# Two small buffers of a hybrid block's memory norm, allocated ahead of the normalized input

## The chip, the core and the metric

The kernel runs on one core of one Trainium2 chip. The metric is the time of one execution in device microseconds, as the median of several runs. One more execution was recorded by the hardware profiler; all rows below come from it. PE is TensorE's matmul stream and PEld its weight loads, DVE is VectorE, ACT is ScalarE, POOL is GpSimd, and SP is the engine that issues the loads of the weights.

## What is computed

Two layers act on 512 tokens of width 1024, with 256 memory tokens. Each layer adds three blocks to `x`:

```python
for l in range(DEPTH):                       # DEPTH = 2
    x = x + hybrid_mixer(rms_norm(x, norm_mix_g[l]), ...)
    x = x + memory_cross_attention(rms_norm(x, norm_xattn_g[l]),
                                   rms_norm(mem, norm_mem_g[l]), ...)
    x = x + conv_gated_mlp(rms_norm(x, norm_ffn_g[l]), ...)
return rms_norm(x, final_norm_g)
```

The mixer projects the normalized input to fourteen groups of columns and feeds three branches: chunked retention, a gated delta rule (a triangular solve and a scan over chunks) and dilated window attention. Three gates of width 1024 weigh their outputs, and `w_out` follows. Cross attention has four heads over the memory. The feed-forward block projects up to 2 x 2816, runs a short causal convolution, multiplies silu of one half by the other, and projects down. All is float32.

## The kernel before

**Split matmuls.** Every float32 operand of a projection is held as two parts in the type fp32r: a rounded high part and the low rest. `mm3` (lines 210 to 213) makes a product of three matmuls: high x high, low x high, high x low. For an activation the parts are `xgh` and `xgl` (normalized input), `mh`/`ml` (merged branches), `rh`/`rl`, `gh`/`gl`, `odil` (branch outputs), `ah`/`al` (feed-forward) and `mgh`/`mgl` (memory). For a weight they are `wh`, made by ScalarE in line 200, and `wl`, made by VectorE in line 201, from a slab `w` that SP loads.

**Which operand moves.** `fm_tile` (line 215) has the weight part as the loaded operand (128 x 128) and streams 512 tokens of the activation past it; `fm_one` uses it for one output tile with one slab, which is 8 x 3 = 24 matmuls, and `fm_group` for four output tiles at once. Its outputs have the names `gate`, `ua`, `uu`, `up`, `g`, `dqk`, `rqk` and `xq` where the activation is `xgh`/`xgl`, and `wo`, `dn`, `dl`, `y`, `xo`, `km` where it is another. `tm_group` (line 260) turns this round: a block of 128 tokens of the activation is the loaded operand, and the weight parts stream. Its outputs are `rva`, `rvb`, `rg`, `z`, `dv` (from `xgh`/`xgl`; the 512 columns of `dv` take every fourth token) and `vm` (from `mgh`/`mgl`). In the trace a matmul is written `out<-moving,loaded` with the names in either order.

**Order.** The instructions are put in order by a scheduler when the program is built; the parts that prepare weights are marked to come first, and the evictions of PSUM soon.

**Places in SBUF.** Single tiles lie in the pool `pp` in the order of their allocation: the constants `c`, the parameters `par`, `xgh` and `xgl` (lines 173, 174), and at line 1094 `mrow` and `mrc`. Behind them come the regions (`r0` to `r10`, `q0` to `q2`) that hold `mh`, `rh`, `ah`, `mgh` and the other large tiles in turn, and then the slabs and small tiles. Each start is rounded up to 32 bytes. `mrc` takes the 1 / rms of the memory tokens by partition, and `mrow` the same by column; `memory_norm` fills them once, in layer 0, and `cross` reads them in both layers.

Of the kernel before, what the change touches and what calls it, by code (L numbers as in the profile page):

```python
# [9 lines left out]
F32 = mybir.dt.float32  # L10
# [8 lines left out]
P = 128  # L19
T = 512  # L20
M = 256
# [78 lines left out]
def tile_hybrid(ctx, tc, xT, memT, pos, wts, cst, kst, prm, rows, outT):  # L100
# [4 lines left out]
    pp = ctx.enter_context(tc.tile_pool(name="pp", bufs=1))  # L105
# [57 lines left out]

    c = pp.tile([P, C_N], F32, name="c")
    par = pp.tile([P, P_N], F32, name="par")
    with tc.high_priority(offset=2000000):
        nc.scalar.dma_start(par[:, :P_GC], prm[:, :P_GC])
    ident = c[:, C_ID:C_ID + P]
# [922 lines left out]

        return Two(mh), Two(ml)

    mrow, mrc = pp.tile([P, M], F32, name="mrow"), pp.tile([P, 2], F32, name="mrc")

    def mem_load(kt):
        mraw = tg(f"mem{kt}", (2, M))
        G.dma_start(mraw, memT[:, kt:kt + 2, :])
        return mraw
# [409 lines left out]
```

## Time and profile before

| | us |
|---|---|
| median of 3 runs | 2123.67 |
| lowest and highest run | 2121.73, 2125.4 |
| the profiled execution | 2123.01 |
| its span, first to last instruction | 2121.2 |

Of the span PE is busy for 98%, its weight loads, which overlap with it, for 81%, DVE for 64%, ACT for 43% and POOL for 20%. The program reads 198.55 MB from HBM, nearly all of it weights, at a mean of 97 GB/s. A matmul's duration in the profile runs from its start to a modelled end, and the next one starts before that; so the sum of durations says little, and the distance from one start to the next says what a matmul costs.

### The profile page before, as it was taken

The page shows a single profiled execution, that of the slowest core. Times are in us where ns is not written, and L with a number is a line of the kernel's source. Part 1 is how long each engine was busy: PE and PEld are TensorE (multiplying, and loading weights), DVE is VectorE, ACT ScalarE, POOL GpSimd, SP SyncE. Part 2 cuts the span into 40 slices and gives each one's busy share as a digit, 9 for nine tenths or more (in the row PEclk, how much of TensorE's full clock was granted, in tenths as well). Part 3 has the DMA queues.
Part 4 walks back from the last instruction along what each step waited for, and adds up shares of the span by engine and source line. Part 5 has one row for each costly group of instructions (what it writes and reads, how often), then busy time and mean ns, then how long its engine had stood idle before and what let it go on. Part 6 is the DMA issues. An engine that isn't in the chain of part 4 may idle for free.

```text
span 2121.2 us, 28468 instructions
## 1 busy us (share of the span) xinstructions
PE 2076.4 (98%) x10537; PEld 1710.2 (81%) x10537; DVE 1363.0 (64%) x2478; ACT 918.7 (43%) x1879; POOL 422.4 (20%) x438
## 2 busy tenths in 40 slices
PE   7999999999999999999999999999999999999997
PEld 6787888777787888888887889888788878888886
DVE  6789666444767875476547986834447677645754
ACT  4653424443445543244445533344335454423433
POOL 6842220013010311011115231200211021101112
PEclk9999999999999999999999999999999999999998
DMA  4332222235232323222332231223342322223232
GB/s 154 125 105 81 77 78 81 79 115 149 86 116 78 100 90 96 98 94 94 119 122 85 95 109 52 74 80 110 110 119 90 109 90 90 92 98 99 90 95 84
DMA packets 64874, 207.32 MB, mean 98 GB/s; under 512 B 7896, under 2 KB 15552, under 8 KB 63968
## 3 DMA queue, kind: packets, MB, share of 16 engines
q1 hardware_dynamic: 60240, 191.89, 28.5%
q0 software_dynamic: 4144, 13.54, 2.2%
q8 instruction: 82, 1.34, 0.3%
q14 instruction: 56, 0.46, 0.1%
q10 hardware_dynamic: 352, 0.09, 0.0%
HBM read 198.55 MB, written 6.93 MB: 97 GB/s over the span
## 4 chain that ended last, share of the span: by engine, by line
PE 84%; DVE 8%; DMA 3%; issue 2%; ACT 2%; POOL 1%; SPq 0%; ACTq 0%; DVEq 0%; POOLq 0%
PE gate L212 4%; PE gate L213 4%; PE gate L211 4%; PE uu L213 4%; PE ua L213 4%; PE ua L212 4%; PE uu L212 4%; PE ua L211 4%; PE uu L211 4%; PE dn L211 3%; PE dn L213 3%; PE dn L212 3%; DVE wl L201 2%; PE dqk L213 2%; PE dqk L212 2%; PE dqk L211 2%
## 5 line engine op out<-in xcount | busy, mean ns | idle before, releaser
L200 ACT ACTIVATE wh<-w 128x512 fp32r<-128x512 f32 (+2 forms) x690 | 429.4, 624 | 844.2 <-PE uu L212 123.0
L201 DVE TENSOR_TENSOR wl<-w,wh 128x512 fp32r<-128x512 f32 (+2 forms) x690 | 512.3, 745 | 335.3 <-ACT wh L200 315.1
L213 PE MATMUL gate<-xgh,wl 128*128 128x512 f32 x384 | 153.5, 400 | 1.4 <-DVE wl L201 1.4
L211 PE MATMUL gate<-xgh,wh 128*128 128x512 f32 x384 | 153.0, 399 | 0.6 <-ACT wh L200 0.6
L212 PE MATMUL gate<-xgl,wh 128*128 128x512 f32 x384 | 152.9, 398 | 0.0
L301 POOL TENSOR_TENSOR acc<-acc,sq 128x512 f32<-128x512 f32 (+1 forms) x48 | 66.1, 1377 | 356.6 <-ACT sq L300 297.7
L211 PE MATMUL ua<-xgh,wh 128*128 128x512 f32 x320 | 126.6, 396 | 0.0
L212 PE MATMUL ua<-xgl,wh 128*128 128x512 f32 x320 | 126.6, 396 | 0.0
L213 PE MATMUL ua<-xgh,wl 128*128 128x512 f32 x320 | 126.6, 396 | 0.0
L211 PE MATMUL uu<-xgh,wh 128*128 128x512 f32 x320 | 126.6, 396 | 0.0
L212 PE MATMUL uu<-xgl,wh 128*128 128x512 f32 x320 | 126.6, 396 | 0.0
L213 PE MATMUL uu<-xgh,wl 128*128 128x512 f32 x320 | 126.6, 396 | 0.0
L1243 POOL TENSOR_TENSOR fya<-fya,fyu 128x512 f32<-128x512 f32 x44 | 73.0, 1659 | 230.3 <-DVE fyu L1226 228.5
L211 PE MATMUL dn<-ah,wh 128*128 128x512 f32 x264 | 102.7, 389 | 0.0
L212 PE MATMUL dn<-al,wh 128*128 128x512 f32 x264 | 102.7, 389 | 0.0
L213 PE MATMUL dn<-ah,wl 128*128 128x512 f32 x264 | 99.8, 389 | 0.0
L213 PEld LDWEIGHTS gate<-xgh,wl 128*128 128x128 f32 x384 | 72.2, 188 | 19.1 <-DVE wl L201 1.9
L212 PEld LDWEIGHTS gate<-xgl,wh 128*128 128x128 f32 x384 | 72.2, 188 | 17.7 <-issue 1.2
L211 PEld LDWEIGHTS gate<-xgh,wh 128*128 128x128 f32 x384 | 72.2, 188 | 17.2 <-ACT wh L200 0.9
L401 POOL TENSOR_TENSOR rot<-rot,tab 128x512 f32<-128x512 f32 x32 | 49.0, 1536 | 175.9 <-DVE rot L400 162.4
L213 PE MATMUL g<-xgh,wl 128*128 128x512 f32 x192 | 77.3, 404 | 3.2 <-DVE wl L201 3.0
L211 PE MATMUL g<-xgh,wh 128*128 128x512 f32 x192 | 77.3, 402 | 1.2 <-ACT wh L200 1.2
(513 smaller groups left out, 5145.1 us busy)
## 6 DMA issues: line engine op xcount, KB each, us to landing
w<-in_wts SPq DMA_DIRECT2D x330, 512.0 KB, 3.5
mem<-in_memT POOLq DMA_DIRECT2D x12, 256.0 KB, 3.4
attn<-gd_rd POOLq DMA_DIRECT2D x2, 1024.0 KB, 5.9
tab<-tabs_d POOLq DMA_DIRECT2D x4, 512.0 KB, 4.2
x<-in_xT SPq DMA_DIRECT2D x2, 1024.0 KB, 6.5
dr<-sh_rd SPq DMA_DIRECT2D x16, 128.0 KB, 4.3
x_d<-x SPq DMA_DIRECT2D x8, 256.0 KB, 4.2
x<-x_d SPq DMA_DIRECT2D x2, 1024.0 KB, 6.7
```

The lines of the kernel that those rows point to most:

```text
L200: S.activation(wh[:, :m], w[:, o:o + m], AF.Copy)
L201: V.tensor_tensor(wl[:, :m], w[:, o:o + m], wh[:, :m], ALU.subtract)
L211: PE.matmul(out, lhsT=lh, rhs=rh, start=start, stop=False)
L212: PE.matmul(out, lhsT=lh, rhs=rl, start=False, stop=False)
L213: PE.matmul(out, lhsT=ll, rhs=rh, start=False, stop=stop)
L301: eng.tensor_tensor(acc, acc, sq, ALU.add)
L401: G.tensor_tensor(t, t, tab[:, 1, :], ALU.mult)
L1243: G.tensor_tensor(ya, ya, yu, ALU.mult)
```

## The change

Line 1094 moves up, to stand in front of `xgh` and `xgl`. What is computed, the names and the shapes stay.

```diff
     c = pp.tile([P, C_N], F32, name="c")
     par = pp.tile([P, P_N], F32, name="par")
+    mrow, mrc = pp.tile([P, M], F32, name="mrow"), pp.tile([P, 2], F32, name="mrc")
     with tc.high_priority(offset=2000000):
         nc.scalar.dma_start(par[:, :P_GC], prm[:, :P_GC])
...
-    mrow, mrc = pp.tile([P, M], F32, name="mrow"), pp.tile([P, 2], F32, name="mrc")
-
     def mem_load(kt):
```

The order of the instructions in the built program is the same on all five engines, row by row, and so are the semaphores that they wait for; only numbers in names and line numbers differ. What differs is the place of four tiles in each partition of SBUF, in bytes from its start:

| tile | bytes | start before | start after | start mod 2048, before and after |
|---|---|---|---|---|
| `c` | 1552 | 16512 | 16512 | |
| `par` | 2080 | 18080 | 18080 | |
| `xgh` | 16384 | 20160 | 21216 | 1728, 736 |
| `xgl` | 16384 | 36544 | 37600 | 1728, 736 |
| `mrow` | 1024 | 52928 | 20160 | |
| `mrc` | 8 | 53952 | 21184 | |
| `r7` (`rh` and others), the first region | 8192 | 53984 | 53984 | 736, 736 |
| `r1` and `r10` (`mh`, `ah` and others) | 8192 | 103136, 140000 | the same | 736, 736 |
| `r5` (`mgh` and others) | 8192 | 86752 | 86752 | 736, 736 |
| `wh`, the first of 3 | 2048 | 164576 | 164576 | 736, 736 |
| `wl`, the first of 3 | 2048 | 170720 | 170720 | 736, 736 |

Within `xgh` and `xgl` the eight slices of 512 tokens are 2048 bytes apart, and so are the slices in the regions; the three `wh` are 2048 bytes apart, and the three `wl`; a load of 128 weights starts at a multiple of 512 bytes in its tile.

## Rows read from the trace of the kernel before

**Rows 1.** The page: busy us (share of the span), and PE's granted clock in 40 slices.

```profile
PE 2076.4 (98%) x10537; PEld 1710.2 (81%) x10537; DVE 1363.0 (64%) x2478; ACT 918.7 (43%) x1879; POOL 422.4 (20%) x438
...
PEclk9999999999999999999999999999999999999998
```

**Rows 2.** PE's waits: line, for what: us in total, times, longest us.

```profile
PE rva L211 <- ACT wh L200: 8.5, 3, 7.9
PE nfin_rp L1206 <- DVE rc L287: 5.2, 2, 4.7
PE g L213 <- DVE wl L201: 3.0, 2, 2.3
PE rg L212 <- DVE wl L201: 2.4, 2, 1.4
PE z L212 <- DVE wl L201: 2.2, 2, 1.6
...
PE xo L211 <- DVE pt L1171: 0.3, 2, 0.2
```

**Rows 3.** PE by windows: us, PE busy (x), PEclk, DMA share, GB/s.

```profile
723.06:728.66 5.60, 5.60 (x25) 1.00 0.33 97
...
568.34:573.78 5.44, 5.44 (x25) 1.00 0.32 99
```

**Rows 4.** Four tiles: duration min/median/max in ns, first and last start, forms.

```profile
L212 PE MATMUL ua<-xgl,wh x320: 395/396/397, 723.3 to 2038.4; 128*128 128x512 f32 x160
...
L211 PE MATMUL wo<-mh,wh x128: 389/389/389, 568.3 to 1648.9; 128*128 128x512 f32 x128
...
L211 PE MATMUL dn<-ah,wh x264: 389/389/395, 823.9 to 2073.7; 128*128 128x512 f32 x132
...
L213 PE MATMUL y<-rh,wl x64: 389/389/501, 350.6 to 1472.2; 128*128 128x512 f32 x64
```

**Rows 5.** Groups of matmuls by shape: xcount | busy us, mean ns | idle before.

```profile
L212 PE MATMUL gate<-xgl,wh 128*128 128x512 f32 x384 | 152.9, 398 | 0.0
...
L212 PE MATMUL ua<-xgl,wh 128*128 128x512 f32 x320 | 126.6, 396 | 0.0
...
L212 PE MATMUL g<-xgl,wh 128*128 128x512 f32 x192 | 76.7, 399 | 0.0
...
L212 PE MATMUL xq<-xgl,wh 128*128 128x512 f32 x64 | 25.5, 398 | 0.0
...
L213 PE MATMUL rg<-wh,xgl 128*128 128x512 f32 x64 | 25.2, 394 | 0.0
```

**Rows 6.** PE by windows: `rg`, `vm`, `rvb`, `km`, `dv`, `rva`.

```profile
1079.89:1088.75 8.86, 8.86 (x39) 1.00 0.31 90
1695.90:1699.76 3.86, 3.86 (x18) 1.00 0.34 98
1159.86:1170.82 10.96, 10.96 (x96) 1.00 0.38 98
611.86:617.73 5.87, 5.87 (x50) 1.00 0.34 96
328.54:336.81 8.27, 8.27 (x36) 1.00 0.42 132
1066.94:1072.91 5.97, 5.97 (x50) 1.00 0.28 89
```

**Rows 7.** All engines by windows: us, then PE, PEld, DVE, ACT, POOL busy.

```profile
116.50:168.00 51.50, 51.06 (x246) 41.63 (x246) 45.66 (x97) 31.90 (x76) 17.23 (x24) 1.00 0.36 109
723.06:823.86 100.80, 100.80 (x433) 81.15 (x432) 76.65 (x116) 47.64 (x75) 18.00 (x31) 1.00 0.30 96
1066.80:1252.00 185.20, 180.63 (x920) 149.14 (x919) 140.86 (x292) 87.07 (x208) 60.11 (x61) 0.99 0.33 102
```

**Rows 8.** All engines in cross attention of layer 0.

```profile
612.00:656.00 44.00, 44.00 (x269) 38.95 (x268) 30.73 (x72) 22.27 (x49) 1.29 (x1) 1.00 0.34 107
```

## The prediction

> **What bounds the kernel now.** I read the page's busy times first, then PE's waits, then the matmuls' groups, and at last single stretches of PE's timeline. PE is busy for 2076.4 of 2121.2 us at a clock that is full nearly throughout [rows 1], and what it waits for is small: the largest wait is the first weight slab (8.5 us), the next the last rms (5.2 us), and then DVE's low weight halves at 3.0 us and less [rows 2]. So the time is the number of matmuls times the distance from one start to the next, and a change that leaves every instruction in its place can move it only by moving that distance.
>
> That distance differs with the operand. In a stretch of `ua` 24 matmuls start in 5.60 us (the row counts 25, as one still runs from before): 233.3 ns from start to start. In a stretch of `wo`, of the same size and at full clock, 24 start in 5.44 us: 226.7 ns [rows 3]. Both have `wh` or `wl` as weights and 512 columns. The records' own durations say the same: 395 to 396 ns wherever `xgh` or `xgl` moves, 389 ns for `mh`, `ah` and `rh` [rows 4]. `xq`, built by the same helper as the last half of `wo`, has a mean of 398 ns, so the loop is not the cause [rows 5].
>
> What sets the tiles apart is their address. From the table of addresses above, `xgh` and `xgl` are the only large operands that begin at 1728 past a multiple of 2048; `wh`, `wl` and every region begin at 736. The difference is 32 modulo 64. It also shows where `xgh` is not the moving operand but the weights: in `rg` 38 matmuls take 8.86 us (233.2 ns), in `vm`, with `mgh` of a region as weights, 17 take 3.86 us (227.1 ns) [rows 6]. Whichever side the odd tile is on, the pair is slow. I read this as two streams, the moving operand of one matmul and the weights of the next, which get in each other's way less where their addresses have the same remainder.
>
> **The change part by part.** No instruction is added, removed or moved on any engine or queue, no semaphore either; two small tiles go to lower addresses and `xgh` and `xgl` up by 1056 bytes, to remainder 736, which is that of `wh`, `wl` and the regions. The terms:
>
> 1. `xgh` or `xgl` moving, 512 columns. Per line there are 384 `gate`, 320 `ua` and as many `uu`, 192 `g` and as many `dqk`, 64 `xq` and as many `rqk` and `up`: 1600, by three lines 4800 [rows 5]. Each goes from 233.3 to 226.7 ns: 4800 x 6.67 ns = 32.0 us less.
> 2. `xgh` or `xgl` as weights under 512 columns, `rg` and `z`, alike: 6 x 64 = 384 [rows 5], from 233.2 to 227.1 ns: 2.3 us less.
> 3. The `dv` group of 512 columns reads its weights with a step of four elements and runs at 8.27 us / 35 = 236.3 ns [rows 6]. No in-step case of it exists in the trace. Between no change and 227.1 ns lie 0 and 192 x 9.2 ns = 1.8 us; I take the middle, 1.0 us less, for want of a nearer row.
> 4. 256 columns, `xgh` as weights: `rvb` 10.96 us / 94 = 116.6 ns (two of the 96 still run from before the stretch). `km`, in step, takes 5.87 us / 49 = 119.8 ns [rows 6]. Here the odd remainder is the faster one. `rvb` and the 256-column `dv` are 384 matmuls: 384 x 3.2 ns = 1.2 us more. `rva`, 264 columns, goes at 5.97 us / 49 = 121.8 ns; scaled from `km`, 119.8 x 264 / 256 = 123.5 ns, so 192 x 1.7 ns = 0.3 us more. The bounds of the two are nothing and twice their sum of 1.5 us.
> 5. The moved `mrow` and `mrc` are read by a few VectorE and ScalarE instructions in cross attention; PE is busy throughout there [rows 8], and I cost this at nothing. If that cover were gone it would still be a handful of instructions. The writes of `xgh` and `xgl` themselves keep shape and place.
>
> The sum is -32.0 - 2.3 - 1.0 + 1.5 = -33.8 us, if all of it is PE's own time.
>
> Some is not. What comes late next is the weight halves: the wait of `g` for `wl` is 3.0 us, of `rg` 2.4, of `z` 2.2 [rows 2]; DVE is busy for 45.66 of 51.50 us in the stretch around `z` and `g`, 89%, but only for 76.65 of 100.80 us in the feed-forward's `ua` and `uu` [rows 7]. In the feed-forward (320 + 320 + 64 per line, 2112 of the 4800) PE waits for nothing and the gain is whole: 14.1 us. In `gate`, `g`, `dqk`, `rqk`, `rg`, `z` and `dv` the terms sum to (1152 + 576 + 576 + 192) x 6.67 ns + 2.3 + 1.0 = 19.9 us, and I let 3 us of those be given back to waits that begin earlier and end as late as now. The bounds are nothing, and a growth by half of all that PE waits for apart from the two ends of the program: the view has 21 rows that sum to 38.3 us, less 8.5 and 5.2 is 24.6, half of it 12 us. I stay near the lower bound because PE idles for only 4.57 of 185.20 us in the second layer's stretch of that kind [rows 7]. So -33.8 + 3.0 = -30.8 us.
>
> **A rule that speaks against it.** The Trainium skill, "TensorE: Matmul & The Clock Gate", Part 2, says that TensorE has two independent SBUF read ports and that loading the next weights takes no bandwidth from the running matmul; "SBUF — State Buffer" (Specifications) gives lines of 16 bytes, of which both remainders are multiples. By these the shift would change nothing and the time would stay at 2123 us. The rows do not show two independent streams: one pair of shapes has two distances, by which tile is in it [rows 3, 4, 6].
>
> **The rivals.** First, no change: the long distance belongs not to the remainder but to something else of `xgh` and `xgl`, above all to their being the lowest large tiles. For it: the trace has no tile of theirs at another remainder and no low tile in step, so it does not part the two. Against it: the step would have to lie between the end of `xgl` (52928) and the start of the first region (53984), where `rh` already has 389 ns [rows 4]. Time: the profiled 2123.0 us.
>
> Second, the bound moves: the pace improves, but in the mixer DVE's halves come no earlier, and all of the 19.9 us there turn into waits. For it: 89% busy on DVE around `g` [rows 7]. Against it: its waits are a few, 3.0 us at most in one group [rows 2], and DVE itself has 11% left, where PE wants 3% more. Then 33.8 - 19.9 = 13.9 us are left: 2109 us.
>
> Third, slower: the remainder matters, but not as "the same is best"; the new place is as bad as the worst that the trace has, the 236.3 ns of `dv` [rows 6]. For it: 256 columns go faster out of step than in step, so one rule for all sizes does not hold. Against it: the tiles that move in `wo` and `dn` have just the remainder that `xgh` gets, with the same weights and shapes. The price is (4800 + 384) x 3.0 ns = 15.6 us: 2139 us. It decides against the change as soon as the new distance is over 234 ns.
>
> **How the numbers follow.** The profiled execution took 2123.0 us, 1.8 us more than its span and 0.7 us under the median of 2123.67; I work from it: 2123.0 - 30.8 = 2092 us. Chances: forecast 0.80, no change 0.09, gain lost to DVE 0.07, slower 0.04. The forecast's own range is 2087 (nothing given back, term 3 whole, term 4 nothing: 36.1 us less) to 2102 us (12 us given back). To hold 8 in 10 it reaches to the second rival, and by 1 us below for the spread of runs: 2086 to 2110 us. What a measurement of this kernel can tell from no change is about 0.2%, 4 us; so faster has 0.87, within 0.2% 0.09, slower 0.04.
>
> **What would show it.** Right: `ua`, `uu`, `gate`, `xq` durations at 389 instead of 396 ns, a `ua` group of 24 in 5.44 instead of 5.60 us, `rg` near 227 ns, `rvb` near 120 ns, each of the four `ua` and `uu` stretches about 3 us shorter, `dn` and `wo` unchanged, and PE's waits a few us larger. Wrong: `ua` still at 395 to 396 ns (first rival), or at 389 ns with PE's waits on `wl` some 15 us up (second), or over 396 ns (third).

## The result and the profile after

The changed kernel takes 2099.55 us (median of 4 runs, 2097.8 to 2103.09) beside 2122.7 us (median of 4, 2119.94 to 2125.4) of the kernel before: a ratio of 0.9893 with a 95% interval of 0.9874 to 0.9912, 23 us faster. The forecast was 2092 us in a range of 2086 to 2110. A second set of runs of the same kernel gave 0.990 (0.9884 to 0.9915). The sign, the bound and the price of a `ua` matmul came as forecast; of the 33.8 us of the terms 10.6 did not arrive, and these are what the later experiments are about.

The profiled execution took 2103.09 us, the slowest of the four, with a span of 2101.3. The page of after, busy us and PE's clock, to be held against [rows 1]:

```profile
PE 2053.1 (98%) x10537; PEld 1713.9 (82%) x10537; DVE 1360.7 (65%) x2478; ACT 918.1 (44%) x1879; POOL 423.2 (20%) x438
...
PEclk9999999999999999999999999999999999999998
```

PE's busy time fell by 23.3 us and its span by 19.9; the 3.4 us between them are time in which PE stands still. The other engines do the same work as before.

**The matmuls.** The durations of `ua` after (ns, min/median/max) answer to [rows 4], where they were 395/396/397:

```profile
L212 PE MATMUL ua<-xgh,wh x320: 389/389/389, 718.0 to 2018.2; 128*128 128x512 f32 x160
...
L213 PE MATMUL ua<-xgl,wh x320: 389/389/389, 718.2 to 2018.4; 128*128 128x512 f32 x160
```

Windows of PE of after, in the order `ua`, `wo`, `rg`, `rvb`, `dv`, `rva`, answer to [rows 3, 6]; the columns are us, PE busy (records), clock, DMA share and GB/s:

```profile
717.96:723.40 5.44, 5.44 (x25) 1.00 0.28 99
564.19:569.63 5.44, 5.44 (x25) 1.00 0.32 99
1068.19:1076.84 8.65, 8.65 (x40) 1.00 0.30 92
1148.53:1159.81 11.28, 11.28 (x97) 1.00 0.41 98
329.70:337.93 8.23, 8.23 (x37) 1.00 0.42 131
1055.43:1061.31 5.88, 5.88 (x51) 1.00 0.29 91
```

24 `ua` matmuls now start in the 5.44 us that `wo` always took: 226.7 ns each, from 233.3. 38 of `rg` take 8.65 us, 227.6 ns, from 233.2. 94 of `rvb` take 11.28 us, 120.0 ns, from 116.6: the one shape that gets slower, as forecast. 35 of `dv` take 8.23 us, 235.1 ns from 236.3. 49 of `rva` take 5.88 us, 120.0 ns from 121.8, where a small loss had been forecast.

**Where the gain is and where it is not.** The order of the instructions is the same, so each can be compared with itself. The table gives by how much the time of a part changed from before to after (negative: shorter), summed over both layers; "projections" is the mixer up to the first `gate`, about 0 to 344.5 and 1066.9 to 1393.5 us of before; the last matmul of the second layer ends the count, so the program's end, which got 0.2 us longer in the profile of after, is not in it. The second column is the sum of the forecast's terms there (for the projections 1344 matmuls x 6.67 ns + 2.3 + 1.0 - 1.5 us); the last two columns are runs of experiments below.

| us | by the terms | after | after, run again | all moved by 256 bytes |
|---|---|---|---|---|
| projections | -10.8 | +4.1 | +3.6 | -0.2 |
| gates to `w_out` | -7.7 | -8.7 | -9.2 | -7.6 |
| cross attention, feed-forward | -15.4 | -15.5 | -13.9 | -15.0 |
| all | -33.8 | -20.2 | -19.5 | -22.8 |

The feed-forward, cross attention and the gates gave what the matmuls alone would give. The projections gave nothing or lost. Their PE waits, in the second layer's stretch (1055.36 to 1384.97 us of after; line, for what: us in total, times, longest):

```profile
PE g L214 <- DVE wl L202: 2.4, 1, 2.4
PE y L570 <- DMA A<-Td: 2.0, 1, 2.0
PE g L212 <- ACT wh L201: 1.9, 2, 1.6
PE rg L213 <- DVE wl L202: 1.4, 1, 1.4
```

and the same of before (1066.9 to 1393.5):

```profile
PE g L213 <- DVE wl L201: 2.3, 1, 2.3
PE rg L212 <- DVE wl L201: 1.4, 1, 1.4
PE g L211 <- ACT wh L200: 0.3, 1, 0.3
```

Two waits are larger or new: `g` for the high half (0.3 to 1.9 us) and `y` for the inverse's blocks that a DMA brings (2.0 us, no such row in this layer before). The waits for the low halves `wl` did not grow: over the whole run their rows sum to 14.2 us before and 10.9 after. Nor is the wait of `y` new to the kernel. In the first layer it was there before, in a row that names GpSimd; but the second load of `A` landed 0.13 us ahead of that `y`, as it landed 0.14 us ahead of the two that waited after:

```profile
PE y L569 <- POOL rot L401: 1.4, 1, 1.4
```

The wait of the second layer on the timeline of after (start, us, engine, line; in brackets the idle time before and what ended it):

```profile
1232.18 2.01 POOL L563 DMA_DIRECT2D T<-Td  x3 [0.95 <-DMA Td<-Tg]
1234.17 2.59 POOL L560 DMA_DIRECT2D A<-Td  x4
...
1238.65 0.39 PE L212 MATMUL dqk<-xgh,wh 128*128 128x512 f32 x1
...
1241.02 0.21 PE L570 MATMUL y<-A 32*32 32x32 f32 x2 [1.98 <-DMA A<-Td]
...
1242.76 0.63 PE L212 MATMUL dqk<-xgh,wh 128*128 128x512 f32 x1
1243.19 0.63 PE L213 MATMUL dqk<-xgl,wh 128*128 128x512 f32 x1
```

GpSimd issues three loads of `T` and four of `A` one after another, 4.6 us in all, behind a transfer through DRAM, and a fixed list of matmuls on PE covers them. In the kernel before the same `y` started at 1250.07 us without a wait. Counted from the start of the store `Td<-Tg`, the last `dqk` ahead of `y` starts after 11.47 us before and after 11.25 us after, so the faster matmuls took 0.2 us of the cover. The second load of `A`, which the first `y` needs, had landed after 11.15 us before, and only after 13.48 us after. Most of the wait is this load, which took 4.05 us from issue to landing before and 6.07 after. All four loads of `A` of the second layer, in the profiles of before, of after and of the kernel moved by 256 bytes:

```profile
DMA to landing us min/median/max: 4.0/4.5/5.3
DMA to landing us min/median/max: 4.5/5.6/6.1
DMA to landing us min/median/max: 4.6/5.2/5.7
```

Ten profiles of this case have their instructions in the same order. In eight of them the second load took 3.7 to 5.0 us, in the two of the change 6.05 and 6.07; in these two the weight slab beside it was issued 0.74 and 0.84 us after the first load of `A`, in the others 1.05 to 1.41. That the slab's transfer holds the load up would fit, but was not tried. The last two rows of the timeline show the second half of the price: `dqk` matmuls now last 0.63 us and start 425 ns apart. The windows of after in which the clock is at half, and then those of before:

```profile
33.70:37.10 3.40, 3.40 (x10) 0.50 0.29 81
74.70:78.10 3.40, 3.40 (x9) 0.51 0.50 154
231.70:235.10 3.40, 3.40 (x44) 0.50 0.00 0
1112.30:1115.70 3.40, 3.40 (x9) 0.50 0.51 154
1242.00:1245.40 3.40, 3.40 (x9) 0.50 0.65 217
```

```profile
21.30:24.70 3.40, 3.40 (x18) 0.51 0.74 240
1123.80:1127.20 3.40, 3.40 (x10) 0.51 0.48 154
```

A granted clock of 0.50 is 1.2 instead of 2.4 GHz. Each of these stretches begins within about 2 us of the end of a time in which PE stood still for about a microsecond or more (0.95 to 2.4 us here); not every such time is followed by one. A stretch costs half of its 3.4 us, 1.7 us. Three more of them are 5 us; with the 3.0 us that the waits of the whole run grew by (41.3 us in 22 rows, from 38.3 in 21), that is 8 of the 13.6 us that separate -33.8 from -20.2.

### The profile page after: what moved, and what is told of

It is laid out like the page before. It is cut to its first block, busy times and chain, and to the rows that moved or that the text cites. A ratio compares the mean times of both kernels' runs of the same rounds, so it can differ in the third digit from the quotient of the medians.

```text
span 2101.3 us, 28468 instructions
## 1 busy us (share of the span) xinstructions
PE 2053.1 (98%) x10537; PEld 1713.9 (82%) x10537; DVE 1360.7 (65%) x2478; ACT 918.1 (44%) x1879; POOL 423.2 (20%) x438
## 4 chain that ended last, share of the span: by engine, by line
PE 83%; DVE 8%; DMA 4%; issue 2%; ACT 2%; POOL 1%; SPq 0%; DVEq 0%; ACTq 0%; POOLq 0%
PE gate L213 4%; PE gate L214 4%; PE gate L212 4%; PE uu L214 3%; PE ua L214 3%; PE uu L213 3%; PE ua L213 3%; PE ua L212 3%; PE uu L212 3%; PE dn L214 3%; PE dn L213 3%; PE dn L212 3%; DVE wl L202 2%; PE dqk L214 2%; PE dqk L213 2%
```

## The experiments

**The remainder.** The prediction's reading was that the moving and the loaded operand want the same remainder, and it gave the difference as "32 modulo 64". Four kernels put other differences between `xgh`/`xgl` and everything that meets them.

The kernel before, with an unused tile of 32 bytes behind `xgh` and `xgl`, ahead of `mrow`:

```diff
+    pp.tile([P, 8], F32, name="gap")
     mrow, mrc = pp.tile([P, M], F32, name="mrow"), pp.tile([P, 2], F32, name="mrc")
```

> The order of before with 32 bytes left empty between xgl and mrow: xgh and xgl stay at 20160 and 36544 (a multiple of 64), and everything behind them, the regions, wh and wl, goes up by 32 to a multiple of 64 as well. Moving and loaded operand now differ by 960 bytes modulo 2048, which is 0 modulo 64 and 64 modulo 128. My theory (moving and loaded operand want the same remainder modulo 64): ua at 389 ns, dn at 389 ns, total near that of the changed kernel, 2100 us. Rival one (what counts is the operand's own address, a start on a multiple of 64 is slow): ua 396 and now dn, wo, y too at 396 ns; 2127 more slow matmuls by 6.67 ns, 14 us more than before, 2137 us. Rival two (the remainders have to be the same modulo 128 or more): ua 396, dn 389, no change, 2123 us. It also tells whether the move of mrow and mrc by itself does anything: here they stay behind xgl.

Measured: 2122.01 us, ratio 0.9979 (0.9969 to 0.9989). `ua` starts every 233.1 to 233.5 ns, `dn` every 226.8. The operands now differ by 960 bytes, which is 0 modulo 64 (and 192 modulo 256). So the same remainder modulo 64 is not enough. Nor is it the address of a tile by itself: `dn`, whose tiles moved by 32 bytes together with the weights, kept its pace.

The changed kernel with the same tile behind `xgl`, which brings back a difference of 32:

```diff
     xgl = pp.tile([P, KT, T], F32R, name="xgl")
+    pp.tile([P, 8], F32, name="gap")
```

> The changed kernel with 32 bytes left empty behind xgl: xgh and xgl stay at 21216 and 37600, everything behind goes up by 32. My theory: ua back at 396 ns, dn still 389 ns, the gain is gone, 2123 us. Rival (own address): ua stays at 389 ns, dn and wo go to 396 ns, 2100 + 14 = 2114 us. Rival (the gain came from where mrow and mrc lie): ua stays at 389 ns and the time at 2100 us.

Measured: 2122.73 us, ratio 0.9986 (0.9975 to 0.9998); `ua` at 395/396/397 ns again, every 233.0 to 233.4 ns. 32 bytes undo the change, with `mrow` and `mrc` in their new place. `xgh` and `xgl` are the lowest large tiles in the changed kernel and here, at the same addresses, and they are fast in the one and slow in the other: the first rival, that the long distance belongs to the lowest tiles, is out, and so is any part of the two small buffers.

Odd places within larger tiles, 16 and 48 bytes, then 8 and 24:

```diff
-    xgh = pp.tile([P, KT, T], F32R, name="xgh")
-    xgl = pp.tile([P, KT, T], F32R, name="xgl")
+    xgh = pp.tile([P, KT * T + 16], F32R, name="xgh")[:, 4:4 + KT * T].rearrange("p (k t) -> p k t", k=KT)
+    xgl = pp.tile([P, KT * T + 16], F32R, name="xgl")[:, 12:12 + KT * T].rearrange("p (k t) -> p k t", k=KT)
```

> The changed kernel with xgh beginning 16 bytes and xgl 48 bytes past the remainder modulo 64 of wh and wl (both tiles 64 bytes longer, the remainders of all other tiles modulo 64 as in the changed kernel). If any difference modulo 64 is slow, all three lines of ua have 396 ns and 233.3 ns from start to start. If only the bit of 32 counts, the lines that move xgh (offset 16) have 226.7 ns and the line that moves xgl (offset 48) 233.3 ns. If the cost grows with the distance to the next multiple of 64, both lie between, near 230 ns.

> As the kernel before it in this list, with xgh 8 bytes and xgl 24 bytes past the common remainder. Any difference slow: 233.3 ns or more on all lines of ua, more if a start inside 16 bytes costs something of its own. Only the bit of 32: 226.7 ns on all lines. Growing with distance: xgh near 228 ns, xgl near 232 ns.

Measured in one execution each: 2124.66 us with `ua` every 232.7 to 232.8 ns, and 2131.35 us with 235.2 (`xgh` and `wh`), 235.6 (`xgl`) and 233.5 ns (`xgh` and `wl`). The differences to the weights are here 112 and 16 bytes, and 120 and 40. There is no gradual approach: 16 bytes apart is as slow as 112. The kernel whose parts start 8 bytes off a multiple of 16 is slower still; whether by the difference or by that start itself, no run parts. The third rival's 234 ns exists, only not at the place that the change chose.

**Modulo what.** Moving `xgl` alone by 128 and all that lies behind by 384 puts `xgh` 384 and `xgl` 256 bytes from the weights:

```diff
     xgh = pp.tile([P, KT, T], F32R, name="xgh")
+    pp.tile([P, 32], F32, name="gap1")
     xgl = pp.tile([P, KT, T], F32R, name="xgl")
+    pp.tile([P, 64], F32, name="gap2")
```

> The changed kernel with empty space behind xgh (128 bytes) and behind xgl (256 bytes): against the weights, xgh is off by 384 bytes (0 modulo 128, 128 modulo 256) and xgl by 256 bytes (0 modulo 256, 256 modulo 512). If the remainders have to agree modulo 128, all lines of ua have 226.7 ns from start to start; if modulo 256, the line that moves xgl is at 226.7 ns and those that move xgh near 233.3 ns; if modulo 512, all are near 233.3 ns and the time is 2122 us.

Measured in one execution: 2110.85 us, between the two kernels. The matmuls that move `xgl` reach the next start in 225.9 ns, those with `xgh` in 232.4 (`wh`) and 228.4 ns (`wl`): 256 apart is fast and 384 is not. It left the mixed series hard to read, since each matmul follows one with the other operand; so two more kernels put both parts at the same distance, one gap of 128 or of 256 bytes behind `xgl`:

> The changed kernel with one unused tile of 128 bytes behind the low part of the normalized input: both its parts stay where they are, and all regions and weight slabs lie 128 bytes higher, so that the moving and the loaded operand differ by 128 modulo 256. If equal remainders modulo 256 are what counts: 512-column matmuls of ua start every 231 to 234 ns and the run takes 2113 to 2124 us. If modulo 128 is enough: 226.7 ns and 2098 to 2105 us.

> The same with 256 bytes: the operands differ by 256. If equal remainders modulo 256 are what counts: ua at 226.7 ns and 2098 to 2106 us, as the change itself. If only equal remainders modulo 512 or more count: 231 to 234 ns and 2113 to 2124 us.

Measured in one execution each, beside 2123.77 us of the kernel before: 2120.3 us at 128 and 2100.47 us at 256. `ua` of the two, a line of the page of each (busy us, mean ns), at 128 first:

```profile
L213 PE MATMUL ua<-xgh,wh 128*128 128x512 f32 x320 | 126.4, 395 | 0.0
```

```profile
L213 PE MATMUL ua<-xgh,wh 128*128 128x512 f32 x320 | 124.5, 389 | 0.0
```

128 bytes apart starts every 232.7 to 233.4 ns, 256 apart every 226.5 to 227.0, like 0. Of the differences tried in both parts, 0 and 256 are fast; 16, 32, 40, 112, 120, 128, 960 and the 992 of before are slow. In all that was run the operands want the same remainder modulo 256.

The last kernel settles a second thing by the way. In its profile, with the same fast matmuls, the second load of `A` took 4.59 us, `y` of the second layer did not wait for it and no stretch at 1.2 GHz followed there; the second layer's projections got 0.6 us shorter, where they got 3.0 us longer in the profile of after. The 3.6 us between the two are the wait of 2.0 us and the 1.7 us behind it.

**Where the rest of the gain went.** The changed kernel was run again as it is, and beside it a pair with the two layouts in which VectorE has less to do in the projections:

> The changed kernel once more, as it is, on the chip and beside the runs of before that the next two kernels have: 2100 us, a ratio of 0.989, 23 us. It fixes the gain that the two lightened kernels are held against.

```diff
-        V.scalar_tensor_tensor(y, cin[:, 1:T + 1], w[:, 1:2], y, ALU.mult, ALU.add)
-        V.scalar_tensor_tensor(y, cin[:, 0:T], w[:, 0:1], y, ALU.mult, ALU.add)
...
-        for j in range(31):
+        for j in range(1):
```

> The order of places of before, with VectorE relieved in the mixer's projections: the forward substitution of the delta rule's inverse makes 1 of its 31 steps, and the convolution of the delta rule leaves out two of its four taps. Beside the next kernel, which differs from it in the addresses alone, it tells where the gain of the change is lost. Theory one (in the mixer's projections the gain turns into waits for VectorE and for the delta rule's chain): here it stays, and this kernel is 28 to 33 us slower than the next. Theory two (the gain is lost on PE itself, to spells at 1.2 GHz and to the matmuls with 256 columns): the two are as far apart as before and the changed kernel, 21 to 25 us.

> The changed kernel's addresses with the same work left out as in the kernel before it in this list. Theory one: 28 to 33 us faster than that, and the stretch of the mixer's projections, which the change left as long as it was (344.5 us in layer 0 before, 345.6 after), is shorter by some 6 us in each layer. Theory two: 21 to 25 us faster, and that stretch as long in the one as in the other, with more or longer spells at 1.2 GHz.

Measured: the changed kernel 2104.09 us, ratio 0.990 (0.9884 to 0.9915). The light pair 2106.0 us with the layout of before (0.9909, 0.9893 to 0.9926) and 2080.02 us with that of after (0.9788, 0.9773 to 0.9802): the change is worth 26.0 us there, beside 21.6 in the full kernel of the same runs. By the pair's spans it is 27.5. That lies between what the two theories gave. The stretches say more than the sum: in the pair the projections of the two layers get 4.1 and 3.1 us shorter, where the full kernel's got 1.1 and 3.0 us longer. Apart from the program's end there is one stretch at 1.2 GHz in the light kernel with before's layout and none with after's; the five of the full kernel's profile are gone. Of the 4.1 and 3.1 us, 7.2 together, 1.7 are that one stretch. The two gains of 26.0 and 21.6 us also stand not far out of the noise, as the runs of one kernel spread over 3 to 6 us. So with that work left out more of the projections' gain stays. Which part of the work matters the pair does not show, since it leaves out the delta rule's chain together with VectorE's instructions, and the waits speak against VectorE as the one cause: PE's rows of waits for VectorE sum to 25 us before and after alike, those for ScalarE to 12.0 and 12.7, those of `y` for `A` to 1.4 and 3.7. In the profile of the change run again the three are 27.0, 13.2 and 3.1 us. 3.6 of the 10.8 us are missing in the light pair too, where the largest waits of PE within the layers are these, in the kernel with after's layout:

```profile
PE rvb L212 <- DVE zgz L427: 3.1, 2, 1.7
PE gk L525 <- DVE A L528: 2.3, 1, 2.3
PE g L212 <- ACT wh L201: 2.2, 3, 1.7
```

**A try at getting it back.** If VectorE is what is late, one tap of the convolution on ScalarE and GpSimd should help:

```diff
-        V.scalar_tensor_tensor(y, cin[:, 1:T + 1], w[:, 1:2], y, ALU.mult, ALU.add)
+        S.activation(z, cin[:, 1:T + 1], AF.Identity, scale=w[:, 1:2])
+        G.tensor_tensor(y, y, z, ALU.add)
```

> The changed kernel with one of the four taps of the delta rule's short convolution taken from VectorE (one multiply-and-add of 512 columns, 12 per layer, about 0.6 us each) and given to ScalarE (multiply) and GpSimd (add). Theory one, that in the mixer's projections the gain turns into waits on VectorE's work and into stretches at 1.2 GHz behind them: VectorE has some 7 us less to do per layer there, a part of the 7 to 10 us that the mixers hold comes back, 2092 to 2100 us beside 2100 to 2104 of the change. Rival, that the waits there are set by GpSimd's queue (the small transfers of the triangular solve are issued on it) or by latency: GpSimd's further 24 additions, about 1 us each, make them longer, 2104 to 2112 us.

Measured: 2111.59 us, ratio 0.9944 (0.993 to 0.9958), some 11 us slower than the change alone. The rival's time came, and the timeline of this kernel shows how its longest new wait arises (POOL, then DVE, then PE):

```profile
80.92 3.42 POOL L498 TENSOR_TENSOR A<-attn,c 128x512 f32<-128x512 f32 x2
84.31 1.27 POOL L503 TENSOR_TENSOR attn<-attn,c 128x512 f32<-128x512 f32 x1
85.53 1.26 POOL L441 TENSOR_TENSOR y<-y,z 128x512 f32<-128x512 f32 x1
```

```profile
86.83 1.73 DVE L442 SCALAR_TENSOR_TENSOR y<-cin,par,y 128x512 f32<-128x512 f32 x1 [3.64 <-POOL y L441]
88.59 0.69 DVE L435 TENSOR_TENSOR cin<-g,nm_row 128x512 f32<-128x512 f32 x1
```

```profile
89.34 0.79 PE L212 MATMUL z<-wh,xgh 128*128 128x512 f32 x1 [4.28 <-DVE cin L435]
```

The moved addition stands in GpSimd's queue behind 4.7 us of work on `A` and `attn`; the last tap on VectorE waits for it, the eviction `cin` waits behind that tap, and `z` on PE waits for `cin`. The granted clock is 0.50 from 88.11 to 94.94 us, and PE works at 1.2 GHz for 5.6 us of these. And VectorE was not relieved: 24 instructions of 0.87 us are 20.8 us less, yet its busy time went from 1360.7 to 1363.8 us. Its other instructions took longer beside GpSimd's further 37.7 us; `wl` is the largest of them (count | busy us, mean ns), after first, then this kernel:

```profile
L202 DVE TENSOR_TENSOR wl<-w,wh 128x512 fp32r<-128x512 f32 (+2 forms) x690 | 511.8, 745 | 333.7 <-ACT wh L201 313.5
```

```profile
L202 DVE TENSOR_TENSOR wl<-w,wh 128x512 fp32r<-128x512 f32 (+2 forms) x690 | 521.6, 759 | 349.9 <-ACT wh L201 331.5
```

The Trainium skill, "SBUF — State Buffer", Who interferes with whom, says that VectorE and GpSimd share one pair of ports under an exclusive lock; that agrees with the longer `wl`, though no run here parts the port from other causes. The kernel's instructions also stand in another order than those of the change, so its 11 us are not the tap's alone. No version tried beats the change.

## Why the prediction was right, and where it was not

**What bounds the kernel: right.** Only the distance between matmuls changed, and the time followed it: the four stretches of `ua` and `uu` got 2.9 to 3.5 us shorter each, as the 3 us forecast, and cross attention and feed-forward together 15.5 us beside 15.4.

**The rule of the remainder: right in kind, too narrow in size.** The rows of before showed one slow pair and several fast ones, which fits any modulus that divides 2048 and is over 32. "32 modulo 64" was the smallest of these and is refuted: 192 and 128 modulo 256 are 0 modulo 64 and slow. The forecast did not depend on it, because the change makes the remainders modulo 2048 equal; a padding made by the rule modulo 64 would have gained next to nothing, as the first experiment did (0.2%). Why 256 counts, no run here shows.

**Terms 1 to 4.** The means here are over distances from start to start with no wait in them. The 6.67 ns per matmul came out in `ua` and `uu` (233.3 to 226.7 ns). `gate` reached 227.6, `g` and `up` some 227.9, `xq` the same, `rqk` 228.2 and `dqk` 228.5, from 233.0 to 233.3 ns: term 1 is 28.0 us instead of 32.0, because one stretch of `ua` and one of `wo` were taken for all. `rg` and `z` gained 4.6 ns in the mean, 1.8 us, where one stretch of `rg` shows 5.6. `dv` gained 1.2 ns, 0.2 us, and not the middle of the two bounds, 1.0: with a step of four elements the remainder hardly matters. `rvb` lost 3.1 ns as forecast and the 256-column `dv` 2.1, 1.0 us together. `rva` was scaled from `km` by its columns, to 123.5 ns, and came out at 120.0, the pace of 256 columns: 0.3 us gained instead of lost. Together that is 29.3 us, where 33.8 were forecast. Why `dqk` stays 1.8 ns above `ua` with the same operands and addresses was not tried.

**Term 5: right.** The small buffers cost nothing; the second experiment has them in the new place and stands 0.1% under the kernel before.

**The step that failed** is "I let 3 us of those be given back to waits", chosen "near the lower bound because PE idles for only 4.57 of 185.20 us in the second layer's stretch". By the medians 6 us of the 29.3 were given back, twice what was taken, within the bounds of 0 to 12; in the profiled execution, which is 3.5 us over the median, 9. With the 4.5 us that the terms were too large, that makes the 7.5 us between 2092 and 2099.55. The same stretch after:

```profile
1055.26:1243.83 188.57, 179.49 (x920) 149.93 (x919) 140.59 (x292) 86.77 (x208) 60.16 (x61) 0.99 0.34 103
```

PE idles for 9.08 us, twice as long [rows 7], and the stretch got 3.4 us longer although its matmuls of 512 columns follow each other faster. The waits as a sum came as costed, 3.0 us more in the profile, but not as the step had them: those for `wl` fell by 3.3 us, and those of `y` for `A` and of `g` for `wh` grew by 2.3 and 2.1. What had no term is the second price of a wait, the 1.7 us at 1.2 GHz behind some of them: three more such stretches are 5 us of the profiled execution. The clock that was granted in each run says how typical that is. In the mean it was 0.9956 over the 35 runs of before that stand beside the experiments (0.993 to 0.997) and 0.9943 over eight runs of the change (0.992 to 0.996). Over 2100 us the difference is, as an estimate, nearly 3 us, between one and two stretches of 1.7. So the median lies in the forecast's own range of 2087 to 2102 us because the bound for waits was wide, not because the clock was thought of (by its own terms that range ends at 2101). The second rival (DVE's halves come no earlier, all of 19.9 us lost in the mixer) was wrong in its sign, 15 us more of waits on `wl`, and in the gates, which lost nothing; but in the profiles of the change the projections did lose all of their 10.8 us.

**What stays open.** Of the 9 us that the profiled execution gave back, 8 have a row; the last one lies in short idle times. What decides how many stretches at 1.2 GHz an execution gets is not settled: the change had five and four in two profiled executions, the kernel moved by 256 bytes three, and the times of 2103.09, 2103.49 and 2100.47 us go with that; the kernels at the old pace had none to three. Nor is it settled why the second load of `A` landed late in the two profiles of the change. That a chain of small transfers, issued later or from another queue, would recover the 2 us of `y` was not tried.

## What to carry to other kernels

Where two groups of matmuls of one shape differ by a few per cent in their distance from start to start, compare the addresses of the moving and of the loaded operand: here equal remainders modulo 256 were worth 6.6 ns of 233 per matmul of 512 columns, and the empty 256 bytes of one kernel cost nothing that its time shows (2100.47 us). At 256 columns it went the other way (120.0 beside 116.6 ns), so measure the shape that dominates. When the bound engine gets faster everywhere, give the slow clock behind its waits a term of its own, and look at chains that show no wait now: the second load of `A` had landed 0.65 us before its `y` began, and its time to landing varied by more than that from profile to profile.

## What the runs showed of the hardware beyond that

- Matmuls of 512 columns in fp32r (`ua`) start every 226.7 ns when the two operands' addresses are equal modulo 256, about every 233 ns at differences of 16, 32, 112, 128 and 192 bytes from that, and up to every 235.6 ns at 40 and 120 bytes, with the parts 8 bytes off a multiple of 16. The Trainium skill, "SBUF — State Buffer", Who interferes with whom, gives PE two independent read ports; the measured distances depend on both addresses together, so here the measurement decides.
- A wait of PE of 2 us could cost 3.7 (2.0 and 1.7): behind some of the waits stood 3.4 us at a granted clock of 0.50. Which ones differs between executions of one kernel (five stretches and four).
- Taking 20.8 us of instructions from VectorE by giving GpSimd 37.7 us left VectorE's busy time where it was (1363.8 beside 1360.7 us).
